# Modulation products in four column groups per weight row tile instead of two

## The chip, the cores and the metric

The kernel runs on one core of one Trainium2 chip. The metric is the device time of one execution in microseconds (us), as the median over runs; a separate execution was recorded by the hardware profiler. Below, PE is TensorE's matmul side and PEld its weight loads, DVE is VectorE, ACT is ScalarE, POOL is GpSimd, and SP is SyncE, whose queue issues the DMAs.

## The reference, cut to what matters

The program is a four-layer network on two streams of 256 tokens (`x`, here "l", and `ctx`, here "c"), width 1024, in float32, followed by a second block of attention branches and a feed-forward stage. Every one of the four layers is modulated by two vectors, `c` for the one stream and `c_ctx` for the other:

```
def modulation(cvec, w_ada, b_ada):
    return jnp.split(jax.nn.silu(cvec) @ w_ada + b_ada, 3, axis=-1)

sh_l, sc_l, gt_l = modulation(c, w_ada, b_ada)
sh_c, sc_c, gt_c = modulation(c_ctx, w_ada, b_ada)
h_l = rmsnorm(x_lat, g_pre) * (1.0 + sc_l[:, None, :]) + sh_l[:, None, :]
h_c = rmsnorm(x_ctx, g_pre) * (1.0 + sc_c) + sh_c
y_l, y_c = mixer(h_l, h_c, need_ctx=need_ctx)
x_lat = x_lat + gt_l[:, None, :] * rmsnorm(y_l, g_post)
```

`w_ada` is 1024 x 3072 for each layer. So a modulation is a product of two rows (the two vectors) with a large matrix: shift and scale are needed before the layer's mixer, the gate after it.

## The kernel before, in words

The modulation product is made on TensorE with the two vectors as the stationary operand. `cs` holds them as 8 row tiles (k = 0 to 7) of 128 features, each padded from 2 to 32 columns, so one product fills only 32 of the array's 128 columns: one of its four column groups. The group is chosen by the 32 PSUM partitions that the product writes. The weight streams through as the moving operand, 512 columns at a time. Each float32 matmul stands in the trace as two records, two passes over the same columns.

**Layers 1 to 3, and the gate of layer 0 (`ada_steps`, L518 to L570).** The weight of a layer comes in blocks of 1024 columns (block 0 and 1: scale and shift of half the features each; block 2: the gate), one DMA of 128 x 1024 (512 KB, tile `ar`, two buffers) for each row tile k. There are ten blocks in all, hence 80 such DMAs and 80 steps. Two row tiles are taken together: when the odd one has come, four matmuls of 512 columns are issued (L537), row tile k-1 into column groups 0 and 1 (for the two halves of the columns), row tile k into groups 2 and 3. So PSUM ends with two partial sums of every column. They are added afterwards: for scale and shift by a copy to SBUF (L541), four transposes (L558, recorded at the helper's line L735), a copy (L560) and an addition (L562); for the gate by two matmuls with a selection matrix `sel` (L548), an addition and a multiplication on DVE (L552, L553) for each half, and a DMA to DRAM.

**Scale and shift of layer 0 (`ada_first`, L490 to L516).** Four groups of 512 columns, each in four DMAs of two row tiles; row tile k goes to column group k mod 4 with 512 columns (L502). PSUM holds four partial sums, added by four transposes and a reduction on DVE (L508).

**Order.** `ada_steps` is a generator. The function that loads a weight part of the main products (`load_part`) advances it by one step (`pump`), so modulation steps are strewn among the main products (`gemm_a` at L377 to L379, `gemm_b` at L388 to L391); before a layer's last normalization the rest is emitted at once (`drain`). The order of the instructions on each engine is not that of the source: the tile framework's planner lists them by when it expects their inputs, earlier source lines first, and inserts the semaphores. On the chip each engine then runs its list in order, and SP its DMA list too. The four matmuls of two row tiles (called a quad below) can therefore be cut apart by other work.

The main products split each weight part into two halves in float32r, one by ACT (L356), one by DVE (L358).

Of the kernel before, what the change touches and what calls it, by code (L numbers as in the profile page):

```python
# [45 lines left out]
# ------------------------------------------------------------------ host layout  # L46
# [14 lines left out]
class Weight:  # L61
    """A weight cut into column blocks and row parts, each contiguous per partition."""
# [151 lines left out]


def _sel():
    """Sums the partial sums of column groups 32 (2 i + h) + v over i, by (h, v)."""
    s = np.zeros((128, 4), np.float32)
    for i in range(2):
        for h in range(2):  # L220
            for v in range(2):
                s[32 * (2 * i + h) + v, 2 * h + v] = 1.0
    return s
# [7 lines left out]
def prep(I):  # L231
# [39 lines left out]
    A["k_sel"] = _sel()  # L271
# [4 lines left out]
# ------------------------------------------------------------------ device  # L276
# [3 lines left out]
class Net:  # L280
# [39 lines left out]
    # --- tiles  # L320
# [49 lines left out]
    def gemm_a(self, ps, xh, xl, parts, KC=8, n0=0, n=None):  # L370
        """ps[tokens, n] += x^T . W: xh(k), xl(k) -> [128, tokens]."""
# [9 lines left out]
    def gemm_b(self, outs, parts, n0, KC=8, m=128):  # L381
        """outs: [(ps[m, tokens], xh, xl)]; W columns n0..n0+m stationary."""
# [10 lines left out]
    # --- small helpers  # L393
# [36 lines left out]
    # --- setup  # L430
# [21 lines left out]
    def setup2(self):  # L452
        nc, A = self.nc, self.A
        self.sel = self.c([128, 4], F32, "sel")
        self.dma(self.sel, A["k_sel"])
# [12 lines left out]
    # --- modulation  # L468
# [15 lines left out]
    def drain(self, upto=None):  # L484
        """Emit the rest of the filler (up to a mark)."""
        for v in self.filler:
            if upto is not None and v == upto:
                break

    def ada_first(self, mod, g):  # L490
        """Scale and shift of the first layer for features 256 g + (0..255); a column group for each of four row tiles."""
        nc = self.nc
        src = self.A["w_l0_mod"]
        ps = self.pt([128, 512], "tp")
        for i, (off, k0, kc, n) in enumerate(WEIGHTS["l0_mod"].off[g]):
# [4 lines left out]
            for k in range(k0, k0 + kc):  # L500
                p = 32 * (k % 4)
                nc.tensor.matmul(ps[p:p + 32, :], self.cs[:, k, :], r[:, k - k0, :], start=k < 4, stop=k > 3)  # L502
        rows = self.mid([128, 512])
        nc.scalar.activation(rows, ps, AF.Copy)
        tp = self.pt([128, 4, 128], "tp")
        self.transposes(tp, rows, 4)
        cp = self.tmp.tile([128, 4, 2], F32, name=self.nm("cp"), tag="cp", bufs=2)
        nc.vector.reduce_sum(cp, tp.rearrange("p j (i v) -> p j v i", i=4)[:, :, 0:2, :], axis=AX)  # L508
        ks = slice(2 * g, 2 * g + 2)
        bcol, gpre = mod["bcol"], mod["gpre"]  # L510
        for i, v in enumerate("cl"):
            t = self.tmp.tile([128, 2], F32, name=self.nm("sc"), tag="sc", bufs=2)
            j = "lc".index(v)
            nc.vector.scalar_tensor_tensor(t, cp[:, 0:2, j], 1.0, bcol[:, 8 + 2 * g:10 + 2 * g], op0=OP.add, op1=OP.add)
            nc.vector.tensor_mul(mod["A"][v][:, ks], t, gpre[:, ks])
            nc.vector.tensor_add(mod["B"][v][:, ks], cp[:, 2:4, j], bcol[:, ks])  # L516

    def ada_steps(self, mod, pairs):  # L518
        """Modulation by pairs of column blocks: 0, 1 (scale, shift) of half the features; 2 gate (to DRAM, by rows).
        The array's four column groups take two blocks of two row tiles at a time."""  # L520
# [4 lines left out]
        for b in pairs:  # L525
            ps = self.pt([128, 512], "tp")
            for off, k, kc, n in w.off[0 if l == 0 else b]:
                r = self.wp.tile([128, 1024], F32, name=self.nm("ar"), tag="ar", bufs=NADA)
                self.dma(r, bass.AP(tensor=src.tensor, offset=src.offset + off, ap=[[n, 128], [1, n]]))
                if k % 2 == 0:  # L530
                    r0 = r
                    yield "part"
                    continue
                for i, x in enumerate((r0, r)):
                    for h in range(2):
                        g = 32 * (2 * i + h)
                        nc.tensor.matmul(ps[g:g + 32, :], self.cs[:, k - 1 + i, :], x[:, h * 512:(h + 1) * 512],  # L537
                                         start=k == 1, stop=k == 7)
                yield "part"
            rows = self.mid([128, 512])  # L540
            nc.scalar.activation(rows, ps, AF.Copy)  # L541
            if b == 2:
                gs = self.pt([64, 512], "tp")
                for h in range(2):
                    row = lambda t: bass.AP(tensor=A[f"l{l}_{t}"].tensor, offset=A[f"l{l}_{t}"].offset + h * 512,
                                            ap=[[0, 2], [1, 512]])
                    o = gs[32 * h:32 * h + 2, :]
                    nc.tensor.matmul(o, self.sel[:, 2 * h:2 * h + 2], rows, start=True, stop=True)  # L548
                    br = self.tmp.tile([2, 2, 512], F32, name=self.nm("br"), tag="big", bufs=2)
                    self.dma(br[:, 0], row("brow"))  # L550
                    self.dma(br[:, 1], row("gpost"))
                    nc.vector.tensor_add(br[:, 0], o, br[:, 0])  # L552
                    nc.vector.tensor_mul(br[:, 0], br[:, 0], br[:, 1])  # L553
# [6 lines left out]
            nc.scalar.activation(cp.rearrange("p j (h v) -> p j h v", h=2),  # L560
                                 tp[:, :, 0:64].rearrange("p j (h v) -> p j h v", h=2)[:, :, :, 0:2], AF.Copy)
            nc.vector.tensor_add(cp.rearrange("p j (h v) -> p j h v", h=2), cp.rearrange("p j (h v) -> p j h v", h=2),  # L562
                                 tp[:, :, 64:128].rearrange("p j (h v) -> p j h v", h=2)[:, :, :, 0:2])
            k0 = b * 4
            for i, v in enumerate("lc"):
                t = self.tmp.tile([128, 4], F32, name=self.nm("sc"), tag="sc", bufs=2)
                nc.vector.scalar_tensor_tensor(t, cp[:, :, i], 1.0, bcol[:, 8 + k0:12 + k0], op0=OP.add, op1=OP.add)
                nc.vector.tensor_mul(mod["A"][v][:, k0:k0 + 4], t, gpre[:, k0:k0 + 4])
                nc.vector.tensor_add(mod["B"][v][:, k0:k0 + 4], cp[:, :, 2 + i], bcol[:, k0:k0 + 4])
# [6 lines left out]
    def gates(self, mod, streams):  # L576
        """gate * g_post on all partitions."""
# [8 lines left out]
    # --- norms  # L586
    def normed(self, s, tag=None):
        """x of stream s over its root mean square."""
# [11 lines left out]
    def turn(self, hT, xn, scale, bias=None, kbs=range(4)):  # L600
        """Two token tiles [128, 1024] -> transposed halves, scale (and bias) by feature."""
# [24 lines left out]
    def finish(self):  # L626
        """Transposes of the last stream's prenorm, behind some work on the first."""
# [1423 lines left out]
```

## Time and profile before

| | |
|---|---|
| median of 3 runs | 1505.53 us (1503.57 to 1510.28) |
| span of the profiled execution, first to last instruction | 1510.7 us |
| PE busy | 1467.2 us (97%) |
| DVE busy | 1050.6 us (70%) |
| ACT busy | 741.5 us (49%) |
| DMA, mean over the span | 134 GB/s, queue of the core at 39.6% of 16 engines |

The profiled execution has no time of its own besides its span, which is 5.2 us above the median of the runs. A busy share is the union of an engine's records; matmul records overlap in the pipeline, so a PE at 97% is a PE with nearly no gaps, not one at its peak. What a piece of work costs PE's list is read from the start of its first record to the start of the next record of other work.

### The profile page before, as it was taken

What the parts mean: (1) busy time and instruction counts of PE and PEld (TensorE: products, weight loads), DVE (VectorE), ACT (ScalarE), POOL (GpSimd) and SP (SyncE); (2) the same over time, 40 slices, a digit from 0 to 9 for tenths busy, and PEclk for the clock granted to TensorE, in tenths of its full rate; (3) what the DMA queues carried; (4) which work ended last, traced back from release to release, by engine and by line L of the source; (5) the groups of instructions that cost most, each with busy time, mean ns of one, the idle gap of its engine ahead of it and who ended that gap; (6) DMA issues with size and microseconds to landing.
All of it is one profiled execution on the core that took longest, in us unless ns stands there. A gap on an engine that the chain in (4) does not pass through costs nothing.

```text
span 1510.7 us, 23597 instructions
## 1 busy us (share of the span) xinstructions
PE 1467.2 (97%) x8973; PEld 1164.3 (77%) x8973; DVE 1050.6 (70%) x2259; ACT 741.5 (49%) x1457; POOL 51.0 (3%) x72
## 2 busy tenths in 40 slices
PE   7999999999999999999999999999999999899999
PEld 3786667578778677787778757767888898799987
DVE  3678774463588564877487657788687786888963
ACT  3645443342356344363454425565565655555542
POOL 0000000000000000010010000000000000211110
PEclk9999999999999999999999999999999999999999
DMA  9501314662321524423323243126534353555552
GB/s 354 168 19 43 126 51 160 214 211 78 105 66 47 182 71 166 154 85 139 125 75 136 85 144 112 57 93 222 189 113 140 126 181 99 199 178 181 171 193 98
DMA packets 62192, 202.32 MB, mean 134 GB/s; under 512 B 9977, under 2 KB 13134, under 8 KB 62078
## 3 DMA queue, kind: packets, MB, share of 16 engines
q1 hardware_dynamic: 62078, 200.80, 39.6%
q8 instruction: 71, 1.16, 0.3%
q14 instruction: 43, 0.35, 0.1%
HBM read 199.67 MB, written 1.11 MB: 133 GB/s over the span
## 4 chain that ended last, share of the span: by engine, by line
PE 83%; DVE 6%; DMA 5%; ACT 3%; issue 3%; POOL 0%; SPq 0%; ACTq 0%; DVEq 0%; POOLq 0%
PE mm L377 11%; PE mm L379 10%; PE mm L378 10%; PE mm L388 7%; PE mm L389 7%; PE mm L391 7%; PE tp L537 5%; PE tp L938 3%; DMA ar<-in_w_l_ada_dram 3%; PE tp L933 3%; PE tp L735 2%; PE S L899 1%; PE S L391 1%; PE S L388 1%; PE S L389 1%
## 5 line engine op out<-in xcount | busy, mean ns | idle before, releaser
L358 DVE TENSOR_TENSOR wl<-wr,wh 128x1024 fp32r<-128x1024 f32 (+5 forms) x168 | 196.7, 1181 | 68.9 <-ACT wh L356 65.4
L356 ACT ACTIVATE wh<-wr 128x1024 fp32r<-128x1024 f32 (+5 forms) x172 | 174.6, 1026 | 89.1 <-PE mm L389 33.3
L388 PE MATMUL mm<-thl,wh 128*128 128x256 f32 x608 | 175.4, 289 | 2.2 <-ACT thl L684 1.3
L391 PE MATMUL mm<-thl,wl 128*128 128x256 f32 x608 | 173.9, 287 | 0.0
L389 PE MATMUL mm<-tll,wh 128*128 128x256 f32 x608 | 173.4, 286 | 0.0
L377 PE MATMUL mm<-wh,thl 128*128 128x512 f32 (+3 forms) x312 | 123.0, 394 | 0.9 <-ACT thl L684 0.9
L378 PE MATMUL mm<-wl,thl 128*128 128x512 f32 (+3 forms) x312 | 123.1, 394 | 0.0
L379 PE MATMUL mm<-wh,tll 128*128 128x512 f32 (+3 forms) x312 | 122.3, 393 | 0.5 <-DVE tll L685 0.5
L388 PEld LDWEIGHTS mm<-thl,wh 128*128 128x128 f32 x608 | 116.2, 191 | 5.0 <-issue 1.6
L389 PEld LDWEIGHTS mm<-tll,wh 128*128 128x128 f32 x608 | 116.3, 191 | 1.1 <-issue 0.8
L391 PEld LDWEIGHTS mm<-thl,wl 128*128 128x128 f32 x608 | 116.0, 191 | 0.7 <-issue 0.3
L377 PE MATMUL mm<-wh,thc 128*128 128x512 f32 (+2 forms) x232 | 92.6, 399 | 2.8 <-DVE thc L618 1.9
L379 PE MATMUL mm<-wh,tlc 128*128 128x512 f32 (+2 forms) x240 | 94.0, 394 | 0.2 <-DVE tlc L791 0.2
L378 PE MATMUL mm<-wl,thc 128*128 128x512 f32 (+2 forms) x232 | 91.7, 397 | 0.0
L537 PE MATMUL tp<-ar,cs 128*32 128x512 f32 x320 | 77.7, 621 | 9.8 <-DMA ar<-in_w_l_ada_dram 9.7
L912 ACT ACTIVATE P<-S,nm 128x512 f32<-128x512 f32 (+1 forms) x96 | 58.7, 615 | 54.6 <-DVE nm L905 48.1
L358 DVE TENSOR_TENSOR wl<-wrd,wh 128x1024 fp32r<-128x1024 f32 x52 | 65.9, 1270 | 26.4 <-ACT wh L356 26.3
L377 PEld LDWEIGHTS mm<-wh,thl 128*128 128x128 f32 x312 | 58.9, 189 | 16.2 <-issue 4.4
L378 PEld LDWEIGHTS mm<-wl,thl 128*128 128x128 f32 x312 | 58.9, 189 | 13.3 <-issue 4.6
L379 PEld LDWEIGHTS mm<-wh,tll 128*128 128x128 f32 x312 | 58.8, 189 | 10.3 <-DVE tll L685 0.9
L356 ACT ACTIVATE wh<-wrd 128x1024 fp32r<-128x1024 f32 x52 | 53.6, 1053 | 25.5 <-PE mm L378 22.5
L388 PE MATMUL mm<-thc,wh 128*128 128x256 f32 (+1 forms) x216 | 65.1, 302 | 0.0
(567 smaller groups left out, 3780.7 us busy)
## 6 DMA issues: line engine op xcount, KB each, us to landing
ar<-in_w_l_ada_dram SPq DMA_DIRECT2D x80, 512.0 KB
wr<-in_w_l_in_dram SPq DMA_DIRECT2D x48, 512.0 KB
wr<-in_w_l_out_dram SPq DMA_DIRECT2D x32, 512.0 KB
wr<-in_w_s_mg_dram SPq DMA_DIRECT2D x24, 512.0 KB
wrd<-in_w_s_down_dram SPq DMA_DIRECT2D x22, 512.0 KB
wrd<-in_w_s_gate_dram SPq DMA_DIRECT2D x20, 512.0 KB
wrd<-in_w_s_up_dram SPq DMA_DIRECT2D x20, 512.0 KB
wr<-in_w_s_br_dram SPq DMA_DIRECT2D x12, 512.0 KB
```

Source lines behind the costliest of these rows:

```text
L356: nc.scalar.activation(hi[:, :kc * n], raw[:, :kc * n], AF.Copy)
L358: eng.tensor_sub(lo[:, :kc * n], raw[:, :kc * n], hi[:, :kc * n].bitcast(F32))
L377: nc.tensor.matmul(ps, xh(kk), wh[:, k, n0:n0 + n], start=kk == 0, stop=False)
L378: nc.tensor.matmul(ps, xh(kk), wl[:, k, n0:n0 + n], start=False, stop=False)
L379: nc.tensor.matmul(ps, xl(kk), wh[:, k, n0:n0 + n], start=False, stop=kk == KC - 1)
L388: nc.tensor.matmul(ps, wh[:, k, n0:n0 + m], xh(kk), start=kk == 0, stop=False)
L389: nc.tensor.matmul(ps, wh[:, k, n0:n0 + m], xl(kk), start=False, stop=False)
L391: nc.tensor.matmul(ps, wl[:, k, n0:n0 + m], xh(kk), start=False, stop=kk == KC - 1)
L537: nc.tensor.matmul(ps[g:g + 32, :], self.cs[:, k - 1 + i, :], x[:, h * 512:(h + 1) * 512], start=k == 1, stop=k == 7)
L912: nc.scalar.activation(p[:, :nk], ps[:, i, :], AF.Exp, scale=scale, bias=nm[:, r:r + 1], accum_out=sm[:, r:r + 1])
L933: nc.tensor.transpose(tp[:, r, :], P[r][:, j * 128:(j + 1) * 128], self.eye)
L938: nc.tensor.matmul(o[i * 64:(i + 1) * 64, kv], vv, pT[:, 2 * i:2 * i + 2, :], start=j == 0, stop=j == nj - 1)
```

## The change

Every row tile now takes all four column groups by itself: 256 columns in each in `ada_steps`, 128 in each in `ada_first`, accumulated over all eight row tiles in the same PSUM places. So there are twice (four times) as many matmuls, each half (a quarter) as wide, and no partial sums are left to add. A step of `ada_steps` issues its four matmuls as soon as its own row tile is there; it no longer waits for the odd one.

Behind the matmuls, `ada_steps` copies 256 columns instead of 512, makes two transposes instead of four and reads scale and shift straight from PSUM. For the gate the two matmuls with `sel` go (and the DMA that loads `sel`); bias and gain are loaded by eight DMAs onto 32 partitions of each group instead of four onto two partitions, added and multiplied once on 128 x 256 instead of twice on 2 x 512, and stored by four DMAs instead of two. `ada_first` makes one transpose instead of four, and no reduction. The number of weight DMAs and of steps stays.

```
 ada_first:
-        ps = self.pt([128, 512], "tp")
+        ps = self.pt([128, 128], "tp")
...
             for k in range(k0, k0 + kc):
-                p = 32 * (k % 4)
-                nc.tensor.matmul(ps[p:p + 32, :], self.cs[:, k, :], r[:, k - k0, :], start=k < 4, stop=k > 3)
-        rows = self.mid([128, 512])
+                for j in range(4):
+                    nc.tensor.matmul(ps[32 * j:32 * j + 32, :], self.cs[:, k, :], r[:, k - k0, j * 128:(j + 1) * 128],
+                                     start=k == 0, stop=k == 7)
+        rows = self.mid([128, 128])
         nc.scalar.activation(rows, ps, AF.Copy)
-        tp = self.pt([128, 4, 128], "tp")
-        self.transposes(tp, rows, 4)
-        cp = self.tmp.tile([128, 4, 2], F32, name=self.nm("cp"), tag="cp", bufs=2)
-        nc.vector.reduce_sum(cp, tp.rearrange("p j (i v) -> p j v i", i=4)[:, :, 0:2, :], axis=AX)
+        tp = self.pt([128, 4, 32], "tp")
+        nc.tensor.transpose(tp.rearrange("p a b -> p (a b)"), rows, self.eye)
...
 ada_steps:
-            ps = self.pt([128, 512], "tp")
+            ps = self.pt([128, 256], "tp")
             for off, k, kc, n in w.off[0 if l == 0 else b]:
...
-                if k % 2 == 0:
-                    r0 = r
-                    yield "part"
-                    continue
-                for i, x in enumerate((r0, r)):
-                    for h in range(2):
-                        g = 32 * (2 * i + h)
-                        nc.tensor.matmul(ps[g:g + 32, :], self.cs[:, k - 1 + i, :], x[:, h * 512:(h + 1) * 512],
-                                         start=k == 1, stop=k == 7)
+                for g in range(4):
+                    nc.tensor.matmul(ps[32 * g:32 * g + 32, :], self.cs[:, k, :], r[:, g * 256:(g + 1) * 256],
+                                     start=k == 0, stop=k == 7)
                 yield "part"
-            rows = self.mid([128, 512])
-            nc.scalar.activation(rows, ps, AF.Copy)
+            rows = self.mid([128, 256])
             if b == 2:
-                gs = self.pt([64, 512], "tp")
-                for h in range(2):
...
-                    nc.tensor.matmul(o, self.sel[:, 2 * h:2 * h + 2], rows, start=True, stop=True)
-                    br = self.tmp.tile([2, 2, 512], F32, name=self.nm("br"), tag="big", bufs=2)
...
-                    self.dma(mod["g"][:, h * 512:(h + 1) * 512], br[:, 0])
+                br = self.tmp.tile([128, 2, 256], F32, name=self.nm("br"), tag="big", bufs=2)
+                for i, t in enumerate(("brow", "gpost")):
+                    for g in range(4):
+                        self.dma(br[32 * g:32 * g + 32, i], bass.AP(tensor=A[f"l{l}_{t}"].tensor,
+                                                                    offset=A[f"l{l}_{t}"].offset + g * 256,
+                                                                    ap=[[0, 32], [1, 256]]))
+                nc.vector.tensor_add(rows, ps, br[:, 0])
+                nc.vector.tensor_mul(rows, rows, br[:, 1])
+                for g in range(4):
+                    self.dma(mod["g"][:, g * 256:(g + 1) * 256], rows[32 * g:32 * g + 2, :])
                 yield "gate"
                 continue
-            tp = self.pt([128, 4, 128], "tp")
-            self.transposes(tp, rows, 4)
-            cp = self.tmp.tile([128, 4, 4], F32, name=self.nm("cp"), tag="cp", bufs=2)
...
+            nc.scalar.activation(rows, ps, AF.Copy)
+            tp = self.pt([128, 2, 128], "tp")
+            self.transposes(tp, rows, 2)
+            cp = tp.rearrange("p j (h g v) -> p h g j v", h=2, g=2)
```

## Rows read from the trace of the kernel before

**Rows 1.** The page: busy shares, the chain by engine, L537 (busy us, mean ns | idle before).

```profile
PE 1467.2 (97%) x8973; PEld 1164.3 (77%) x8973; DVE 1050.6 (70%) x2259; ACT 741.5 (49%) x1457; POOL 51.0 (3%) x72
...
PE 83%; DVE 6%; DMA 5%; ACT 3%; issue 3%; POOL 0%; SPq 0%; ACTq 0%; DVEq 0%; POOLq 0%
...
L537 PE MATMUL tp<-ar,cs 128*32 128x512 f32 x320 | 77.7, 621 | 9.8 <-DMA ar<-in_w_l_ada_dram 9.7
```

**Rows 2.** Busy time by stage: stretch, us, PE PEld DVE ACT POOL, clock, DMA, GB/s.

```profile
248.00:300.00 52.00, 49.14 (x216) 28.51 (x214) 24.91 (x55) 18.02 (x31) 0.00 (x0) 1.00 0.63 218
```

**Rows 3.** Timeline of PE, 270 to 273 us: start, length, line, operation, shapes, records.

```profile
270.66 0.39 PE L377 MATMUL mm<-Q,thc 128*128 128x512 f32 x1
270.89 0.40 PE L378 MATMUL mm<-P,thc 128*128 128x512 f32 x1
271.21 1.05 PE L537 MATMUL tp<-ar,cs 128*32 128x512 f32 x4
272.20 0.50 PE L379 MATMUL mm<-Q,tlc 128*128 128x512 f32 x1
...
272.53 0.39 PE L377 MATMUL mm<-Q,thc 128*128 128x512 f32 x1
```

**Rows 4.** Timeline of PE, 248 to 250 us.

```profile
248.48 1.06 PE L537 MATMUL tp<-ar,cs 128*32 128x512 f32 x8
...
249.47 0.50 PE L377 MATMUL mm<-wh,thc 128*128 128x512 f32 x1
```

**Rows 5.** Timeline of PE: the first three stretches, and the last of L537.

```profile
152.74 1.04 PE L537 MATMUL tp<-ar,cs 128*32 128x512 f32 x2
153.72 1.08 PE L938 MATMUL tp<-T,V 128*64 128x256 f32 x8
154.73 1.06 PE L537 MATMUL tp<-ar,cs 128*32 128x512 f32 x6
...
887.32 1.05 PE L537 MATMUL tp<-ar,cs 128*32 128x512 f32 x4
```

**Rows 6.** Timeline of PE, 1078 to 1081 us: another product in four column groups.

```profile
1078.34 1.91 PE L1674 MATMUL S<-w,oh 128*32 128x256 f32 x32
1080.18 0.39 PE L388 MATMUL mm<-thl,wh 128*128 128x256 f32 x1
```

**Rows 7.** Timeline of PE, 223 to 225 us: a gate's first selection product.

```profile
223.39 1.02 PE L548 MATMUL tp<-mid,sel 128*2 128x512 f32 x2
224.34 1.08 PE L938 MATMUL tp<-T,V 128*64 128x256 f32 x8
```

**Rows 8.** The chain that ended last, 28 to 29 us: start, us, what.

```profile
28.49 0.44 PE tp L735 x4
```

**Rows 9.** Timeline of PE, 30 to 32 us: a part of layer 0.

```profile
30.43 1.05 PE L502 MATMUL tp<-P,cs 128*32 128x512 f32 x4
31.41 0.50 PE L379 MATMUL S<-wh,tll 128*128 128x512 f32 x1
```

**Rows 10.** Timeline of the start: the first group's last part, copy, and what follows.

```profile
11.36 1.67 PE L502 MATMUL tp<-Z,cs 128*32 128x512 f32 x4
...
13.08 0.60 ACT L504 ACTIVATE mid<-tp 128x512 f32<-128x512 f32 x1 [6.24 <-PE tp L502]
...
16.69 0.80 PE L377 MATMUL mm<-wh,thc 128*128 128x512 f32 x1 [1.87 <-DVE thc L618]
```

**Rows 11.** Waits of all engines: who, for what, us in total, times, longest.

```profile
PE tp L537 <- DMA ar<-in_w_l_ada_dram: 9.7, 6, 2.7
```

**Rows 12.** Timeline, 270 to 276 us: the DMA issues of `ar`, and PE's next stretch.

```profile
270.44 2.20 SPq L395 DMA_DIRECT2D ar<-in_w_l_ada_dram  x2
...
275.67 1.05 PE L537 MATMUL tp<-ar,cs 128*32 128x512 f32 x4
```

**Rows 13.** SP's own waits: who, for what, us in total, times, longest.

```profile
SPq L367 <- DVE wl L358: 673.0, 170, 61.3
```

**Rows 14.** Instructions of L541: duration ns min/median/max, first and last start.

```profile
L541 ACT ACTIVATE mid<-tp x10: 589/598/607, 220.6 to 914.7; 128x512 f32<-128x512 f32 x10
```

More of the change, by code (lines that the diff above doesn't have):

```diff
@@ L213, in _blockdiag @@
     return (np.arange(128)[:, None] // 16 == np.arange(8)[None, :]).astype(np.float32)
-def _sel():
-    s = np.zeros((128, 4), np.float32)
-    for i in range(2):
-        for h in range(2):
-            for v in range(2):
-                s[32 * (2 * i + h) + v, 2 * h + v] = 1.0
-    return s
 def _any_cmp():
@@ L270, in prep @@
     A["k_mask"] = _masks()
-    A["k_sel"] = _sel()
     A["k_eye"] = np.eye(128, dtype=np.float32)
@@ L453, in setup2 @@
         nc, A = self.nc, self.A
-        self.sel = self.c([128, 4], F32, "sel")
-        self.dma(self.sel, A["k_sel"])
         self.rope = self.c([128, 2, 2, 64], F32, "rope")
@@ L500, in ada_first @@
             for k in range(k0, k0 + kc):
-                p = 32 * (k % 4)
-                nc.tensor.matmul(ps[p:p + 32, :], self.cs[:, k, :], r[:, k - k0, :], start=k < 4, stop=k > 3)
-        rows = self.mid([128, 512])
+                for j in range(4):
+                    nc.tensor.matmul(ps[32 * j:32 * j + 32, :], self.cs[:, k, :], r[:, k - k0, j * 128:(j + 1) * 128],
+                                     start=k == 0, stop=k == 7)
+        rows = self.mid([128, 128])
         nc.scalar.activation(rows, ps, AF.Copy)
-        tp = self.pt([128, 4, 128], "tp")
-        self.transposes(tp, rows, 4)
-        cp = self.tmp.tile([128, 4, 2], F32, name=self.nm("cp"), tag="cp", bufs=2)
-        nc.vector.reduce_sum(cp, tp.rearrange("p j (i v) -> p j v i", i=4)[:, :, 0:2, :], axis=AX)
+        tp = self.pt([128, 4, 32], "tp")
+        nc.tensor.transpose(tp.rearrange("p a b -> p (a b)"), rows, self.eye)
         ks = slice(2 * g, 2 * g + 2)
         bcol, gpre = mod["bcol"], mod["gpre"]
-        for i, v in enumerate("cl"):
+        for v in "cl":
             t = self.tmp.tile([128, 2], F32, name=self.nm("sc"), tag="sc", bufs=2)
             j = "lc".index(v)
-            nc.vector.scalar_tensor_tensor(t, cp[:, 0:2, j], 1.0, bcol[:, 8 + 2 * g:10 + 2 * g], op0=OP.add, op1=OP.add)
+            nc.vector.scalar_tensor_tensor(t, tp[:, 0:2, j], 1.0, bcol[:, 8 + 2 * g:10 + 2 * g], op0=OP.add, op1=OP.add)
             nc.vector.tensor_mul(mod["A"][v][:, ks], t, gpre[:, ks])
-            nc.vector.tensor_add(mod["B"][v][:, ks], cp[:, 2:4, j], bcol[:, ks])
+            nc.vector.tensor_add(mod["B"][v][:, ks], tp[:, 2:4, j], bcol[:, ks])
     def ada_steps(self, mod, pairs):
@@ L539, in ada_steps @@
                 yield "part"
-            rows = self.mid([128, 512])
-            nc.scalar.activation(rows, ps, AF.Copy)
+            rows = self.mid([128, 256])
             if b == 2:
-                gs = self.pt([64, 512], "tp")
[L544 to L547, printed above, removed]
-                    nc.tensor.matmul(o, self.sel[:, 2 * h:2 * h + 2], rows, start=True, stop=True)
-                    br = self.tmp.tile([2, 2, 512], F32, name=self.nm("br"), tag="big", bufs=2)
[L550 to L553, printed above, removed]
-                    self.dma(mod["g"][:, h * 512:(h + 1) * 512], br[:, 0])
+                br = self.tmp.tile([128, 2, 256], F32, name=self.nm("br"), tag="big", bufs=2)
[8 more added lines that the diff above has]
+                    self.dma(mod["g"][:, g * 256:(g + 1) * 256], rows[32 * g:32 * g + 2, :])
@@ L555, in ada_steps @@
                 yield "gate"
                 continue
-            tp = self.pt([128, 4, 128], "tp")
-            self.transposes(tp, rows, 4)
-            cp = self.tmp.tile([128, 4, 4], F32, name=self.nm("cp"), tag="cp", bufs=2)
[L560 to L563, printed above, removed]
+            nc.scalar.activation(rows, ps, AF.Copy)
@@ L564, in ada_steps @@
+            tp = self.pt([128, 2, 128], "tp")
+            self.transposes(tp, rows, 2)
+            cp = tp.rearrange("p j (h g v) -> p h g j v", h=2, g=2)
+            pair = lambda x: x.rearrange("p (g j) -> p g j", g=2)
             k0 = b * 4
@@ L566, in ada_steps @@
                 t = self.tmp.tile([128, 4], F32, name=self.nm("sc"), tag="sc", bufs=2)
-                nc.vector.scalar_tensor_tensor(t, cp[:, :, i], 1.0, bcol[:, 8 + k0:12 + k0], op0=OP.add, op1=OP.add)
+                nc.vector.scalar_tensor_tensor(pair(t), cp[:, 0, :, :, i], 1.0, pair(bcol[:, 8 + k0:12 + k0]),
+                                               op0=OP.add, op1=OP.add)
                 nc.vector.tensor_mul(mod["A"][v][:, k0:k0 + 4], t, gpre[:, k0:k0 + 4])
-                nc.vector.tensor_add(mod["B"][v][:, k0:k0 + 4], cp[:, :, 2 + i], bcol[:, k0:k0 + 4])
+                nc.vector.tensor_add(pair(mod["B"][v][:, k0:k0 + 4]), cp[:, 1, :, :, i], pair(bcol[:, k0:k0 + 4]))
     def ada_all(self, mod, nxt):
```

## The prediction

> **What bounds the kernel now.** The page comes first [rows 1]. PE has records for 97% of the span, the chain that ended last runs 83% of its time over PE, and DVE (70%) and ACT (49%) have room. So time taken from PE's list should come off the end, unless PE then meets another wait. L537, the product that is changed, covers 77.7 us, and PE stands idle 9.8 us before it, for DMAs. The table by stage says the same of a stage rich in modulation steps [rows 2]: of 52.0 us PE is busy 49.1, DVE 24.9, ACT 18.0, and the DMA engines move 218 GB/s at a share of 0.63. Last I read PE's timeline, because a mean of 621 ns for overlapping records tells nothing of what a step costs. There the reader should look at differences of starts.
>
> **What a step costs now.** In [rows 3] a half quad (one row tile, two matmuls, four records) starts at 271.21 and the next work at 272.20: 0.99 us. A whole quad takes as long, 248.48 to 249.47 [rows 4], and so does one matmul alone, 152.74 to 153.72 [rows 5]. So a stretch costs two passes of 512 columns, however many of the four groups work in it. Around it the list loses a little more: main products of the same shape follow each other at 0.23 us, but the stretch starts 0.32 after the one before it, and the product behind it needs 0.33. That is 0.09 + 0.10 = 0.19 us for each stretch, at every change between products on the whole array and on one group.
>
> I counted the stretches in the timeline, from the one at 152.74 to the one at 887.32 [rows 5]: 73 for 40 quads. 21 quads run as two half quads, each when its row tile has come; 7 are cut after their first matmul, as at 152.74; 12 run whole, or nearly so, tangled with L548.
>
> **What a step will cost.** The trace of before holds the very shape: L1674 runs 128 x 256 through four column groups of 32. Its last 32 records, four row tiles, take 1.84 us to the next work, 1078.34 to 1080.18 [rows 6], which is at most 0.46 for a row tile. With L537's 0.99 for two passes and some 0.13 of it fixed (two passes at 0.43 would be 0.86), one row tile alone should take 0.13 + 0.43 = 0.56; I take 0.57. Neither more matmuls nor more weight loads show a price here: 32 records in 1.84 us are 57 ns each. The Trainium skill (TensorE: Matmul & The Clock Gate, "Wait — 56ns, not 53.3ns?") puts about 62 ns of sequencer time on each matmul where its hardware decoder is off; by that, eight records would take an estimated 0.50 us, still under 0.57. The trace stays below that figure.
>
> **The sum, part by part.**
> - 42 half quads: (0.99 - 0.57) x 42 = 17.6 us less. Bounds 0 (if DMA sets the pace, below) and 17.6.
> - 7 cut quads: now two stretches each, 2 x 0.99 + 2 x 0.19 = 2.36. As two row tiles 2 x (0.57 + 0.19) = 1.52, and 2.28 if one of them is cut too. That gives 0.6 to 5.9 less; I take 3.
> - 12 whole quads: 0.99 + 0.19 now. Two row tiles in one stretch cost the same (0.57 + 0.43 + 0.19); apart they cost 1.52, 0.34 more. Bounds 0 and 4 more; I take 2 more, since each row tile now has its own place in the source.
> - DMA waits: PE already waits 6 times for `ar` [rows 11]. In such a loop (two steps, two buffers) what PE saves is only waited longer: 6 x 2 x 0.42 = 5 us at most, of which about 4 given back. Other loops have a cushion: SP issues two loads from 270.44 and PE uses the first at 275.67, 5.2 us later, with no wait [rows 12]. Bound: all 17.6 given back.
> - Gate: eight L548 matmuls leave PE. One alone costs 223.39 to 224.34 = 0.95 [rows 7]; one tangled with a quad adds at least a pass of 0.43. 3.4 to 7.6 less; most stand alone, I take 7.
> - Transposes: 6 blocks lose two each, 4 groups of layer 0 three each, 24 in all. Four take 0.44 on the chain [rows 8]: 2.6 less.
> - Layer 0's products: 12 parts follow the first group's four. A part takes 0.98 now, 30.43 to 31.41 [rows 9]. It becomes two row tiles, each two passes of 128 columns: as many columns as one step of 256, so 0.57. 12 x 0.41 = 4.9 less. No row shows four groups at 128 columns; at the densest rate that a row shows, 57 ns a record, the 16 records would take 0.92 and save 0.7. I take 4.9, because [rows 6] is as well explained by columns alone, and keep 0.7.
> - The start: from the last part's matmuls to PE's first main product it takes 11.36 to 16.69 [rows 10]. The matmuls (1.72 to ACT's copy) halve, the copy (0.60) is cut to a quarter of its columns, three transposes go: up to 1.7 less, none if the weight split beside them ends last. I take 1.1.
> - ACT and DVE: ten copies of 512 columns, 0.60 each [rows 14], become six of 256; copies and additions of partial sums go. Nothing of this is on a path where PE is at 97%, so I count no gain for it; were ACT the bound, it would be some 4 us. A gate has 12 small DMAs instead of 6 (eight loads and four stores for four and two), 24 more issues on SP in all; SP spends 673 us waiting for DVE to free weight buffers [rows 13], and that wait covers them. At 2.2 us for two issues (with a wait between them) [rows 12] they would be at most 26 us of SP's time; I cost them at 0.
>
> 17.6 + 3 - 2 - 4 + 7 + 2.6 + 4.9 + 1.1 = 30.2 us. PE is 83% of the chain, so between 0.83 and all of it should reach the end; I take 0.9, which is 27 us. The profiled span is 1510.7, hence 1484 for a profile. The median of the runs lies 5.2 below the span: 1505.5 - 27 = 1478 us.
>
> **Rivals.**
> - *DMA sets the pace.* Every step needs 512 KB through two buffers. If the cushion of 5.2 us is thin, each of the 42 gains turns into a wait: 30.2 - 13.6 = 16.6, times 0.9 is 15, so 1490. For it: PE waits 9.7 us already [rows 11]. Against it: only 6 waits in 80 steps, and a buffer is freed 0.4 us sooner too. Chance 0.12.
> - *PE's freed time meets other waits.* The main products need splits by ACT and DVE and buffers. If PE only idles longer there, the time stays at 1500 to 1508. For it: SP waits on DVE's splits 170 times [rows 13]. Against it: DVE is at 0.48 in [rows 2]. Chance 0.11.
> - *Narrow products are bound by issue.* At 57 ns a record layer 0 saves 0.7 and not 4.9: 1482. The skill's 62 ns (page and section above) would make the 16 records an estimated 0.99 and save nothing, 1482 as well. Chance 0.1, inside the forecast's own range.
> - *Cuts* (slower). A step now has four matmuls, so three seams instead of one, where the planner can put other work. A cut costs a further stretch, 0.57 + 0.19 = 0.76 us. The 27 us are gone at 36 cuts of 80 steps, and 46 make the kernel slower by over 0.5%; 60 would give 1505.5 - 27 + 46 = 1524. For it: 7 of 40 quads are cut today, and each time after the first matmul, which is now shorter. Against it: the four become ready together and stand next to each other in the source, and cuts come only while attention work is about. The skill (TensorEngine Tiling (Array Packing), "Key Properties") says that a change of tiling mode drains the engine, so it speaks for few stretches; the 0.19 us beside each [rows 3] agrees. Chance 0.06.
> - *The groups don't overlap.* Then a step would take 4 x 0.43 = 1.7 us. [Rows 6] exclude it.
>
> **How the numbers follow.** The forecast (1465 to 1490) has 0.71, the issue rival being part of it; DMA pace 0.12 (1485 to 1497), other waits 0.11, cuts 0.06. With all terms at their good ends the gain is 17.6 + 5.9 + 7.6 + 2.6 + 4.9 + 1.7 = 40, so 1465. At the other end DMA pace with the poor ends of gate and layer 0 leaves some 8 us, 1497. Outside 1465 to 1497 I leave the last two rivals and a little, 0.2. A measurement of this kernel tells about 0.5%, 7.5 us, from no change. Faster by more than that (under 1498): 0.71 + 0.1 of the DMA case = 0.81. Within: the rest of it and nearly all of the other waits, 0.13. Slower: 0.06.
>
> **What would show it.** L537's successor: 640 records in 75 to 95 stretches of about 0.57 us each, busy near 55 us. L548 gone; part stretches of L502's successor at 0.57 (0.9 if issue binds). PE idle before the steps at most 15 us; 25 or more means DMA pace. Over 100 stretches mean cuts. If PE's busy time falls by 25 us or more and the span does not, the freed time met other waits. I am wrong if the planner's new list differs far from the old one outside these steps: its luck is no term of the sum.

## The result, and the profile after

The changed kernel takes 1472.3 us, the median of four runs (1471.9 to 1472.6); beside it the kernel before took 1507.2 (1503.6 to 1510.3). The ratio is 0.977 (95% interval 0.974 to 0.980): 34.9 us faster by the medians, where 27 were forecast. The profiled spans differ by 39.9 us (1510.7 to 1470.8).

The page after, against [rows 1]: the span, the busy shares and the chain by engine. PE still has records for 97% of the span, with 33.4 us less of them; DVE and ACT have as much to do as before, in a shorter span.

```profile
span 1470.8 us, 24541 instructions
...
PE 1433.8 (97%) x9445; PEld 1171.0 (80%) x9445; DVE 1046.3 (71%) x2241; ACT 737.2 (50%) x1447; POOL 50.3 (3%) x72
...
PE 86%; DMA 5%; DVE 5%; ACT 2%; issue 1%; POOL 0%; SPq 0%; ACTq 0%; DVEq 0%; POOLq 0%
```

The groups of instructions by line and shape (busy us, mean ns | idle before). L518 is the step's product, L537 in [rows 1]: twice as many records, busy 57.3 us for 77.7. L490 is layer 0's.

```profile
L518 PE MATMUL tp<-ar,cs 128*32 128x256 f32 x640 | 57.3, 398 | 7.1 <-DMA ar<-in_w_l_ada_dram 7.0
...
L490 PE MATMUL tp<-P,cs 128*32 128x128 f32 x128 | 6.6, 313 | 7.6 <-DMA P<-in_w_l_mod_dram 7.6
```

The waits of all engines (us, times, longest), against [rows 11]. The reader should compare with 9.7 us there: PE waits less for `ar`, not more.

```profile
PE tp L518 <- DMA ar<-in_w_l_ada_dram: 7.0, 8, 2.8
```

A stage of the changed kernel that begins in the same loop as that of [rows 2] (us, then busy PE, PEld, DVE, ACT, POOL, clock, DMA share, GB/s). It holds more work, 167 records of main products for 138, so only its shares compare: PE is busy for 0.99 of it, for 0.95 before.

```profile
239.00:289.00 50.00, 49.49 (x293) 33.78 (x292) 29.22 (x60) 21.85 (x37) 0.00 (x0) 1.00 0.70 244
```

PE's timeline of the changed kernel: a part of layer 0 (24.13), two steps in one stretch (240.35), single steps (246.10 with a wait, 251.53), and the DMA issues between them.

```profile
15.71 0.79 PE L366 MATMUL mm<-wh,thc 128*128 128x512 f32 x1 [1.57 <-DVE thc L595]
...
24.13 0.65 PE L490 MATMUL tp<-Z,cs 128*32 128x128 f32 x16
24.70 0.50 PE L368 MATMUL mm<-wh,tll 128*128 128x512 f32 x1
...
240.35 1.07 PE L518 MATMUL tp<-ar,cs 128*32 128x256 f32 x16
241.35 0.50 PE L366 MATMUL mm<-wh,thc 128*128 128x512 f32 x1
...
246.10 0.64 PE L518 MATMUL tp<-ar,cs 128*32 128x256 f32 x8 [0.37 <-DMA ar<-in_w_l_ada_dram]
246.66 0.50 PE L366 MATMUL mm<-wh,thc 128*128 128x512 f32 x1
246.79 2.25 SPq L384 DMA_DIRECT2D ar<-in_w_l_ada_dram  x2
...
251.53 0.64 PE L518 MATMUL tp<-ar,cs 128*32 128x256 f32 x8
252.10 0.50 PE L368 MATMUL mm<-wh,tlc 128*128 128x512 f32 x1
```

Read as differences of starts, a step alone costs 251.53 to 252.10 = 0.57 us and two in one stretch 240.35 to 241.35 = 1.00, where a half quad cost 0.99 [rows 3] and a whole one 0.99 [rows 4]. The steps make 78 stretches: 45 of one step at 0.57, 8 of two at 1.00, the rest cut ones. Layer 0's part takes 24.13 to 24.70 = 0.57 instead of 0.98 [rows 9]. PE's first main product starts at 15.71 instead of 16.69 [rows 10].

PE's whole list, start to start and by kind, accounts for the 39.9 us. The steps' products went from 72.8 to 51.8 us (21.0), layer 0's from 17.6 to 11.3 (6.3), the gate's selection products from 4.8 to nothing. The transposes of the modulation lost 2.3: the six blocks of `ada_steps` went from 2.1 to 1.0 us, layer 0's four from 1.8 to 0.6. The rows show one block before (0.36 us by starts) and one after (0.13). PE's idle time fell from 39.8 to 33.2 (6.6), 2.7 of it before the steps. That is 41.0. Work that the change does not touch gave 1.1 back, in small differences of both signs.

```profile
267.18 0.60 PE L735 MATMUL tp<-eye,mid 128*128 128x128 f32 x4
267.54 0.48 PE L378 MATMUL mm<-wl,thc 128*128 128x512 f32 x1
...
252.91 0.38 PE L712 MATMUL tp<-eye,mid 128*128 128x128 f32 x2
253.04 0.47 PE L368 MATMUL mm<-wh,tlc 128*128 128x512 f32 x1
```

Part of the 39.9 is the clock. Up to their last few microseconds, the profiled executions have the granted clock at its lower level (0.50, 1.2 GHz) for 20.5 us before (from 16.07, 401.77, 872.81 and 1023.00) and for 10.2 us after (from 381.88, 398.94 and 586.68). At that level a half quad takes 873.64 to 875.49 = 1.85 us, for 0.99 at the full clock [rows 3], as these rows of the kernel before show:

```profile
872.81:876.22 3.41, 3.41 (x9) 1.00 (x8) 0.52 (x1) 1.66 (x4) 0.00 (x0) 0.50 0.45 157
...
873.64 1.92 PE L537 MATMUL tp<-ar,cs 128*32 128x512 f32 x4
875.49 0.79 PE L378 MATMUL mm<-wl,thl 128*128 128x512 f32 x1
```

Half of the 10.3 us between the two, some 5 us as an estimate, is the price of the lower clock. The spans differ by as much more than the medians do (39.9 for 34.9).

By time the gain does not come evenly. At the start of the layer-3 stage (858.4 before, 831.1 after) it is 27.3 us; at the same weight part further on (986.7 before, 948.0 after) it is 38.7, and at the end 39.9. So more than a quarter comes in one stretch of layer 3. Half of that (5.6) has come by 877.0 of the changed kernel, with the last steps, and an estimated 1.7 of it is the lower clock from 872.81 above. The other half (5.7) comes behind, where the last gate's tail stands. The experiments go into that.

### The profile page after: what moved, and what is told of

The parts are those of the page before. It is cut to its first block, busy times and chain, and to the rows that moved or that the text cites. A ratio compares the mean times of both kernels' runs of the same rounds, so it can differ in the third digit from the quotient of the medians.

```text
span 1470.8 us, 24541 instructions
## 1 busy us (share of the span) xinstructions
PE 1433.8 (97%) x9445; PEld 1171.0 (80%) x9445; DVE 1046.3 (71%) x2241; ACT 737.2 (50%) x1447; POOL 50.3 (3%) x72
## 4 chain that ended last, share of the span: by engine, by line
PE 86%; DMA 5%; DVE 5%; ACT 2%; issue 1%; POOL 0%; SPq 0%; ACTq 0%; DVEq 0%; POOLq 0%
PE mm L366 11%; PE mm L368 11%; PE mm L367 11%; PE mm L377 8%; PE mm L378 7%; PE mm L380 7%; DMA ar<-in_w_l_ada_dram 3%; PE tp L518 3%; PE tp L915 3%; PE tp L910 3%; PE tp L712 2%; PE S L876 1%; PE S L380 1%; PE S L377 1%; PE S L378 1%
## 5 line engine op out<-in xcount | busy, mean ns | idle before, releaser
L380 PE MATMUL mm<-thc,wl 128*128 128x256 f32 (+1 forms) x216 | 64.8, 300 | 0.0
```

Source lines behind the costliest of these rows:

```text
L380: nc.tensor.matmul(ps, wl[:, k, n0:n0 + m], xh(kk), start=False, stop=kk == KC - 1)
```

## The experiments

Each was timed against the kernel before, in runs on the same chip (median 1506.5 to 1507.4 there). "Price" below is what a run takes over the changed kernel's 1472.3, beside which the kernel before took 1507.2.

**Layer 0 alone** (e1_first_as_before). `ada_first` as it was, the rest as changed.

```
-                for j in range(4):
-                    nc.tensor.matmul(ps[32 * j:32 * j + 32, :], self.cs[:, k, :], r[:, k - k0, j * 128:(j + 1) * 128],
-                                     start=k == 0, stop=k == 7)
+                p = 32 * (k % 4)
+                nc.tensor.matmul(ps[p:p + 32, :], self.cs[:, k, :], r[:, k - k0, :], start=k < 4, stop=k > 3)
```

> The changed kernel, with the products of layer 0 (the function ada_first) as they were before: 512 columns in one group per row tile, four transposes, a reduction. Theory (PE's list: what is taken from PE's list comes off the end, one to one, and a stretch costs the columns that a row tile streams, plus a fixed part): the trace shows 17.6 us for the old products and 11.3 for the new, and PE's 12 transposes more are some 1 us; with ACT's longer copy at the start 7 to 8 us slower than the changed kernel, about 1480. Rival (the planner's luck: the new list merely fell into fewer waits): parts don't add up, anything from 1469 to 1490. Rival (tile by tile, below): nothing, within 2 of 1472, since layer 0 waits for no pair before or after.

1479.7 us (ratio 0.982, 0.981 to 0.984), a price of 7.4. That is inside the theory's 7 to 8: layer 0's part is worth what the columns say.

**The column groups, or the step by row tile?** (e2_two_groups) The new order of steps (each row tile for itself, no partial sums), but two groups of 512 columns; what follows the products is fitted to two groups.

```
-                for g in range(4):
-                    nc.tensor.matmul(ps[32 * g:32 * g + 32, :], self.cs[:, k, :], r[:, g * 256:(g + 1) * 256],
+                for g in range(2):
+                    nc.tensor.matmul(ps[32 * g:32 * g + 32, :], self.cs[:, k, :], r[:, g * 512:(g + 1) * 512],
```

> The changed kernel, but each step of ada_steps uses only two column groups, 512 columns in each, still one row tile at a time and without partial sums, so all else of the change stays (no selection product, early issue, direct reads). Theory (PE's list): a step's stretch is 0.98 us instead of 0.57 and two row tiles in one stretch are 1.85 instead of 1.00: 27 to 33 us more of PE's list, so 1499 to 1505. Rival (tile by tile: the gain comes from issuing each row tile's product as its own tile comes, from freeing its buffer at once and from the missing partial sums, and the groups don't matter): 1472 to 1477.

1511.7 us (ratio 1.003, 1.002 to 1.005). All of the gain is gone and a little more, and the time lies above the theory's 1499 to 1505; the groups line shows why (busy 94.9 us, and start to start 89.3 instead of 51.8):

```profile
L518 PE MATMUL tp<-ar,cs 128*32 128x512 f32 x320 | 94.9, 606 | 9.8 <-DMA ar<-in_w_l_ada_dram 9.6
```

The price is 39.4 us for 37.5 us of PE's list. So it is the four groups that save, and the step by row tile costs without them.

**Does PE's time count one to one?** (e3_twice) Every step's matmul twice, with the vectors halved (and layer 0's sums doubled).

```
-                for g in range(4):
-                    nc.tensor.matmul(ps[32 * g:32 * g + 32, :], self.cs[:, k, :], r[:, g * 256:(g + 1) * 256],
-                                     start=k == 0, stop=k == 7)
+                for i in range(2):
+                    for g in range(4):
+                        nc.tensor.matmul(ps[32 * g:32 * g + 32, :], self.cs[:, k, :], r[:, g * 256:(g + 1) * 256],
+                                         start=k + i == 0, stop=k + i == 8)
```

> The changed kernel with every matmul of a modulation step made twice into the same sums, the two vectors halved to make up for it: twice the streamed columns, the same DMAs, waits and tail. Theory (PE's list, one to one): a step's stretch grows by two passes of four times 256 columns, 0.43 us, so 80 x 0.43 = 34 us more, 1506. Rival (PE's time in these stages is partly hidden behind DMA waits or other engines, as the factor of 0.9 assumed and more): under 17 us more, below 1489.

1510.1 us, a price of 37.8 for 35.1 us more in PE's list. The waits rise with it:

```profile
PE tp L519 <- DMA ar<-in_w_l_ada_dram: 12.8, 15, 1.9
```

One to one, and nothing of it hidden. Longer steps bring more waiting for `ar`, not less (12.8 us for 7.0). A buffer is freed later, and so its next load starts later: before it issues loads, SP waits for the step's products 62 times in the changed kernel, as its own waits show, and the issue at 246.79 above comes right behind a step. That this alone makes the difference was not tested.

```profile
SPq L384 <- PE tp L518: 164.3, 62, 30.5
```

**Two row tiles in one stretch** (e6_pairs). The step waits for the odd row tile again, and issues the eight matmuls of both behind each other.

```
+                if k % 2 == 0:
+                    r0 = r
+                    yield "part"
+                    continue
+                for kk, x in ((k, r), (k - 1, r0)):
+                    for g in range(4):
+                        nc.tensor.matmul(ps[32 * g:32 * g + 32, :], self.cs[:, kk, :], x[:, g * 256:(g + 1) * 256],
+                                         start=kk == 1, stop=kk == 6)
```

> The changed kernel, but two row tiles are issued together when the odd one has come, the odd one first, so that eight matmuls in four groups make one stretch: some 45 stretches instead of 78. Theory (PE's list, each stretch having a fixed part of 0.14 us and 0.19 at its edges): 40 x 1.00 + cuts 5 + 45 x 0.19 = 54 us against 51.8 + 78 x 0.19 = 66.6, so up to 12 us faster than the changed kernel, 1461, less what PE then waits for two loads that start together. Rival (buffers set the pace: both buffers come free together, so each pair waits for a round trip): PE idle before the steps rises from 7 to 25 us or more and the time to 1475 or above.

1464.5 us (ratio 0.973, 0.971 to 0.974): 7.8 us faster than the changed kernel, and the best of all. There are 49 stretches instead of 78, 31 of them of two steps at 1.00; the steps' products take 45.0 us of the list (51.8 in the changed kernel), and the waits for `ar` do not rise:

```profile
L523 PE MATMUL tp<-ar,cs 128*32 128x256 f32 x640 | 48.4, 386 | 5.8 <-DMA ar<-in_w_l_ada_dram 5.5
```

**The gate's old tail** (e5_gate_product). The changed kernel with the copy by ACT, the products that gather the sums on two partitions, and DVE's operations on 2 x 512, in all four layers.

```
-                nc.vector.tensor_add(rows, ps, br[:, 0])
-                nc.vector.tensor_mul(rows, rows, br[:, 1])
+                nc.scalar.activation(rows, ps, AF.Copy)
+                gs = self.pt([64, 512], "tp")
...
+                        nc.tensor.matmul(o[:, e * 256:(e + 1) * 256], self.eye[:, 32 * g:32 * g + 2], rows,
+                                         start=True, stop=True)
...
+                    nc.vector.tensor_add(br[:, 0], o, br[:, 0])
+                    nc.vector.tensor_mul(br[:, 0], br[:, 0], br[:, 1])
```

> The changed kernel with the gate's old tail put back: a copy by ACT, four selection matmuls of 256 columns with two stationary columns, additions and multiplications on two partitions, six small DMAs a gate instead of twelve. Theory (PE's list): 16 matmuls, each 0.35 to 0.55 us of PE's list: 5 to 9 us slower than the changed kernel, 1477 to 1481. Rival (the gate's tail is off the path, and its small DMAs cost what its matmuls gave): within 2 of 1472, or faster if the 24 small DMAs less free SP.

1491.6 us (1486.8 to 1496.2), a price of 19.3; the profiled span is 14.1 longer. Both expectations are missed, since the products take only 5.3 us of PE's list. The list names two more parts of the 14.1: PE idles 5.0 us more (38.2 for 33.2), and the steps take 2.0 more (53.8 for 51.8), cut into 85 stretches for 78. By time, 5 of the 14 come before layer 3's tail and 9 between 893 and 1001 us.

**The steps alone** (e7_steps_alone). `ada_first` and the gate's tail both as before.

> The changed kernel with layer 0's products as before and the gate's old tail (selection products of 256 columns): of the change only the four-group products of ada_steps and their direct reads of scale and shift are left. Theory (parts add up): 1472.3 + 7.4 (layer 0) + 19.3 (gate's tail) = 1499, so the steps themselves are worth about 8 us of the 34. Rival (the trace's account of PE's list, in which the steps' matmuls take 21 us less than before): 1483 to 1488, so the gate's tail put back costs less here than it did alone.

1495.2 us (1493.4 to 1502.4), between the two expectations: 11.4 below the kernel before on that chip. The prices of the two other parts, 7.4 and 19.3, do not quite add: together they cost 22.9. By the medians, then, steps alone are worth 11 us, and the gate and layer 0, on top of them, 23. The profiled spans divide otherwise: 1510.7 before, 1492.5 here, 1470.8 changed, so 18.2 and 21.7. Here the granted clock is at its lower level for 23.9 us, counted as above, where it was 20.5 before and 10.2 in the changed kernel. With half of these taken off, as an estimate for an even clock, the steps alone are worth some 20 us and the rest 15.

**Is it where the tail stands?** (e8_gate_other_bank, e9_before_other_bank) With the old tail the last gate's copy is made at 887.8 us and its selection product only at 941.9. Here its product has PSUM buffers `mm` instead of `tp`, in the changed kernel with the old tail and in the kernel before.

```
-                gs = self.pt([64, 512], "tp")
+                gs = self.pt([64, 512], "mm")
```

> The kernel with the gate's old tail put back (e5_gate_product), but its products go to a PSUM tile of another set of banks (mm) than the transposes' (tp). Same instructions, other place in the lists: the last gate's additions stand near 1190 in DVE's list instead of near 1260. Theory (the old tail costs little work but waits for a bank of tp, and so lands among layer 3's query splits on DVE): the place is what cost, 1475 to 1480. Rival (its work costs, wherever it stands): 1487 to 1494 as with e5_gate_product.

> The kernel before, with nothing changed but the PSUM tile of the gate's selection products, which is taken from the banks mm instead of tp. Theory (place of the gate's tail): 5 to 12 us faster than before, 1495 to 1502. Rival (the tail's work, and the steps): 1504 to 1509, as before.

1496.1 and 1516.4 us (ratio of the second to before 1.007, 1.005 to 1.008): both above the ranges of theory and rival. PE's timeline of the first shows a stall that neither theory had, in layer 2, and the second has the same of 12.2 us at its place:

```profile
573.74 0.28 PE L1197 MATMUL mm<-thl,wl 128*128 128x256 f32 x1
586.23 0.80 PE L1288 MATMUL S<-bb,eye 128*128 128x512 f32 x1 [12.22 <-DVE bb L1222]
```

The planner had put a product that needs DVE's `bb` here; in e5_gate_product that product starts only at 631.8, without a wait. So the two runs say nothing of the last tail. They do show what the order of a list can cost: for the name of a buffer a stall of 12 us, and 9.9 us of time on the kernel before. The next two (e10_last_gate_bank, e11_before_last_bank) change it in the last layer only (`"mm" if l == 3 else "tp"`).

> The changed kernel with the gate's old tail in all four layers, but the last layer's selection products in PSUM buffers mm instead of tp, the other three as in e5_gate_product. The trace of e5_gate_product has the last layer's copy of the gate's sums at 887.8 us and the selection product only at 941.9, so a buffer mid is held for 54 us; behind it PE idles 2.07 us for DVE's mid at 949.0. e8 moved all four tails and met one new stall of 12.2 us at 586 us, in layer 2, which says nothing of the last layer. Theory: it is the late last tail that costs the 9 us between 893 and 1001 us: 1480 to 1484. Rival: the old tail's work costs the same wherever it stands: 1489 to 1493.

> The kernel before with the last layer's selection products in PSUM buffers mm instead of tp, nothing else. There the copy of the last gate's sums is at 914.7 us and the selection product at 967.0, 52 us later. Theory (the late last tail costs about 9 us): 1495 to 1500. Rival (it costs nothing there): 1504 to 1508.

1487.3 and 1507.0 us (ratio of the second to before 1.0005, 0.999 to 1.002). In the first the last tail is now done at once, as its timeline shows:

```profile
892.32 0.39 ACT L523 ACTIVATE mid<-tp 128x256 f32<-128x256 f32 x1
...
892.79 1.02 PE L531 MATMUL mm<-mid,eye 128*2 128x256 f32 x4
...
898.62 0.68 DVE L537 TENSOR_TENSOR br<-br 2x512 f32<-2x512 f32 x1
```

and still the price is 15.0 us, between the two expectations. So the late place does not explain the price, and on the kernel before it costs nothing that the runs can tell. The loss has moved: between 839 and 909 us, around its new place, 8.6 us are lost against the same work in the changed kernel, 2.7 of them ahead of the copy at 892.3, and behind it none.

**The last gate alone** (e12_last_gate_old). The old tail in layer 3, the new one in the others.

```
+                if l == 3:
+                    nc.scalar.activation(rows, ps, AF.Copy)
+                    gs = self.pt([64, 512], "tp")
...
+                    yield "gate"
+                    continue
```

> The changed kernel with the gate's old tail in the last layer alone. Theory (the last tail stands late and holds a buffer): 9 to 10 us over the changed kernel, 1480 to 1484. Rival (each of the four gates carries a like share of the 19 us that all four old tails cost): 1474 to 1478.

1486.5 us (1483.4 to 1489.7), a price of 14.2 (10.9 in the profile) of the 19.3 for all four, above the range of either expectation. That most of it is the last layer's is confirmed. The windows of both kernels between the same two weight parts show how (us, then busy PE, PEld, DVE, ACT, POOL, clock, DMA share, GB/s). First the changed kernel, in which PE has hardly a gap and DVE is busy for 0.86 and 0.83 of the time:

```profile
893.00:948.00 55.00, 54.76 (x391) 42.03 (x390) 47.42 (x108) 32.20 (x70) 0.00 (x0) 1.00 0.23 77
948.00:988.00 40.00, 39.83 (x245) 25.84 (x244) 33.23 (x71) 23.62 (x49) 0.00 (x0) 1.00 0.37 118
```

Then the one with the last gate's old tail, in which PE idles 2.1 and 2.6 us and the granted clock falls to means of 0.97 and 0.96:

```profile
892.00:954.00 62.00, 59.93 (x412) 45.46 (x411) 49.86 (x111) 33.29 (x71) 0.00 (x0) 0.97 0.21 70
954.00:996.00 42.00, 39.40 (x229) 25.06 (x228) 32.80 (x69) 22.80 (x47) 0.00 (x0) 0.96 0.35 108
```

Its timeline names the gaps, behind the tail and on work of the layer itself (in brackets the idle time before, and what ended it):

```profile
931.27 0.59 PE L532 MATMUL tp<-mid,eye 128*2 128x256 f32 x2
...
937.13 0.68 DVE L538 TENSOR_TENSOR br<-br 2x512 f32<-2x512 f32 x1
...
942.12 0.38 PE L377 MATMUL mm<-thl,wh 128*128 128x256 f32 x1 [2.07 <-DVE mid L767]
...
972.89 0.50 PE L895 MATMUL S<-K,Q 128*128 128x512 f32 x1 [1.72 <-ACT P L908]
...
977.42 0.65 PE L934 MATMUL tp<-T,V 128*64 128x256 f32 x4 [0.78 <-DVE T L727]
```

And the windows of 2 us around the first gap (the columns as above) show what follows it:

```profile
938.00:940.00 2.00, 2.00 (x14) 1.36 (x13) 1.92 (x4) 0.46 (x2) 0.00 (x0) 1.00 0.01 2
940.00:942.00 2.00, 0.04 (x1) 0.00 (x0) 1.97 (x5) 0.65 (x2) 0.00 (x0) 1.00 0.00 0
942.00:944.00 2.00, 1.88 (x8) 1.25 (x8) 1.75 (x5) 1.42 (x5) 0.00 (x0) 0.79 0.00 0
944.00:946.00 2.00, 2.00 (x10) 1.82 (x10) 1.45 (x6) 0.60 (x2) 0.00 (x0) 0.50 0.00 0
946.00:948.00 2.00, 2.00 (x15) 1.73 (x15) 1.46 (x6) 1.86 (x8) 0.00 (x0) 0.86 0.02 2
```

PE idles from 940 to 942 while DVE is busy throughout. When it works again, the granted clock is full at first and then 0.50, the level of 1.2 GHz, until about 946.6; the same follows the gap at 972.9. Together the two windows are 9.0 us longer than the changed kernel's (104.0 for 95.0). The products take 2.0 of that in PE's list, and PE idles 4.3 more (4.7 for 0.4). The rest, 2.7, is about what the lower clock costs: an estimated 3, from two stretches of 3.4 us at half speed.

Not every such gap is followed by the lower clock. In e5_gate_product PE idles the same 2.07 us for the same product, and the clock stays full behind it:

```profile
948.98 0.38 PE L377 MATMUL mm<-thl,wh 128*128 128x256 f32 x1 [2.07 <-DVE mid L754]
...
949.00:951.00 2.00, 2.00 (x12) 1.42 (x13) 1.75 (x4) 1.29 (x5) 0.00 (x0) 1.00 0.03 8
951.00:953.00 2.00, 2.00 (x17) 1.84 (x16) 2.00 (x8) 1.28 (x4) 0.00 (x0) 1.00 0.00 0
```

**DVE's share of it** (e13_last_dve). The changed kernel, with the old tail's four DVE operations and their loads beside the new tail in the last layer. Their result is read by nobody.

```
+                    for h in range(2):
+                        b2 = self.tmp.tile([2, 2, 512], F32, name=self.nm("b2"), tag="big", bufs=2)
...
+                        nc.vector.tensor_add(b2[:, 0], b2[:, 0], b2[:, 1])
+                        nc.vector.tensor_mul(b2[:, 0], b2[:, 0], b2[:, 1])
```

> The changed kernel with its new gate tail, and in the last layer beside it the old tail's DVE work alone: four operations on 2 x 512 (0.68 us each, 2.7 together) with their four DMA loads, whose result nobody reads; no copy by ACT and no selection product. DVE is busy 47.4 of 55 us in the stretch behind the tail. Theory (the old tail costs through DVE, which paces that stage): at least half of what the whole old tail costs there, 1479 to 1486. Rival (it costs through the product and the copy on PE's and ACT's lists, or through where those cut the list): 1472 to 1475.

1473.9 us (1473.5 to 1476.8), a price of 1.6 (4.2 in the profiled execution, the slowest of the five). So DVE's 2.7 us of work alone do not cost 14 where the planner put them here, from 872.8 to 880.9. In e12_last_gate_old the same operations ran from 933.5 to 937.8, shortly before PE's wait of 2.07 us for a busy DVE. DVE's work at that late place was not tested.

## Why the prediction was right, and where its terms were off

The direction, the mechanism and the range were right; the forecast of 1478 was 6 us too high. Term by term:

- **Steps (17.6 + 3 - 2 = 18.6).** The cost of a row tile, taken from another product [rows 6] as 0.57, is 0.57, and the 78 stretches lie in the 75 to 95 foreseen. PE's list lost 21.0, an estimated 1.3 of it by the lower clock. That four groups are what saves is shown by the run with two of them.
- **PE's time at 0.9.** The factor was too low: doubling the steps cost 37.8 us for 35.1 us of list. The rival that freed time meets other waits falls with it. The 5.2 us between the span and the median of the kernel before, which the prediction's 1484 for a profile carries over, belonged to that one execution: the changed kernel's span, 1470.8, lies 1.5 below its median.
- **DMA waits (4 given back).** Wrong in sign. The waits fell by 2.7, and rose by 5.8 when the steps were doubled. The term lets the loads come at their own pace; but a load starts when the step has freed its buffer, so a shorter step brings its successor's data sooner. The prediction has this among its reasons against the DMA rival (a buffer freed 0.4 us sooner), but not in the sum. The DMA rival falls by the same numbers.
- **Gate (7).** This is the term that failed most. PE's list lost the 4.8 us of its products, within the bounds; but putting the old tail back costs 19.3 us, or 15.5 on a kernel with layer 0 as before (22.9 - 7.4). What failed is the pricing by PE's list alone, with the copy, the buffers and what the tail holds up at 0. The runs place most of it in layer 3 (14.2 of 19.3) and take away two explanations, the late place of the tail and DVE's work at an early one. What is left is the product with its copy, in PE's and ACT's lists, DVE's work at the late place, and how these shift the order around them. How 2.0 us of products become 11 is seen in the trace as gaps and a lower clock behind the tail. Why the planner's list is that much worse was not settled; e9_before_other_bank shows that lists differ by 10 us for less.
- **Transposes (2.6).** They lost 2.3, close to the term. The blocks of `ada_steps` gave 1.1 of it and layer 0's 1.2.
- **Layer 0 and the start (4.9 + 1.1).** 6.3 in the list and 7.4 in the time. The part of 16 records takes 0.57, which is 36 ns a record. So the rival of products bound by issue falls: the 57 ns of [rows 6] were columns. The Trainium skill (TensorE: Matmul & The Clock Gate, "Wait — 56ns, not 53.3ns?") puts 62 ns of sequencer on a matmul with its hardware decoder off; 36 ns a record is well under that.
- **Cuts.** 78 stretches against 73 before. A seam between two stretches has its price, though, and the run with two row tiles in one shows it: 29 stretches fewer save 6.8 us of list and 7.8 us of time. The Trainium skill's drain at a change of tiling mode (TensorEngine Tiling (Array Packing), "Key Properties") points the same way; here a stretch more costs 0.57 + 0.57 - 1.00 = 0.14 us inside, beside the edges of [rows 3].

By the end, then, the mechanism held and some of the nearness was luck. The sum of 30.2 had 14.6 us for the steps (18.6 less the 4 for waits) and 15.6 for the rest. By the medians these are worth 11.4 and 22.9, errors of opposite signs that nearly cancel; with the lower clock taken out of the profiled spans, an estimate, they are some 20 and 15, and the error is mostly in the wait term. The runs do not settle which of the two splits holds.

## What to carry to other kernels

Where a stationary operand is narrow, as here with 32 columns, try giving every moving tile all four column groups, and keep the matmuls of several tiles together in one stretch: here the stretch had a fixed price beside its columns. Price a wait on a buffer with the loop that frees it, since work that gets shorter also frees it sooner. And price a small side computation by a run, not by its length in the busiest engine's list; with a planner's list, a variant of one buffer's name tells how much of a difference is only order. Before two profiled spans are compared, compare how long the granted clock stood at its lower level in each.

## What the runs showed of the hardware

Four column groups at 128 columns take 16 records in 0.57 us at the full granted clock, 36 ns each; at 256 columns 16 records take 1.00 us, 63 ns each. So the time of a stretch goes by its columns down to that width, plus a fixed part: the first step of a stretch costs 0.57 us, the second 0.43.

Idle time on PE can cost more than itself. In e12_last_gate_old each of the two windows with 2.1 and 2.6 us of idle time holds a stretch at the lower level of the granted clock, behind work that ran at the full one. In the changed kernel the same stage has no such gap, and the granted clock stays at 1.00. It is no rule for a single gap: in e5_gate_product the clock stays at 1.00 behind the same gap of 2.07 us. At the lower level a half quad of the kernel before took 1.85 us, at the full one 0.99.
